# The first loads and the first products of a two-layer encoder kernel: x in 256-column pieces on ScalarE's queue, and another order of the first transposes and products

## The chip, the core and the metric

The kernel runs on one core of a Trainium2 chip. A core has five engines that matter here: TensorE does the matrix products, VectorE and ScalarE work on tiles elementwise, GpSimd does small odd jobs, and SyncE only issues DMAs. ScalarE can issue DMAs too, from a queue of its own; the profile calls a queue's own work ACTq or SPq. The metric is device time in microseconds (us) of one execution, lower is better, and the kernel must compute what the reference computes.

## The reference

An encoder trunk over one sequence: x has 256 tokens and 1024 channels, float32, and there are two layers. Each layer is a token mixer and a gated MLP, both with a root-mean-square norm ahead and a residual add behind:

```python
for layer in range(DEPTH):
    h = h + _token_mixer(_rmsnorm(h, norm1[layer]), w_in[layer], ...)
    h = h + _conv_ffn(_rmsnorm(h, norm2[layer]), w_up[layer], ...)
return _rmsnorm(h, norm_f)
...
u, q, k, v, g_pool, g_attn = jnp.split(xn @ w_in, SPLITS, axis=-1)
```

What matters for this change is the very first thing that the first layer needs: the attention values v, that is, the normed x times the columns of `w_in[0]` that belong to v. They fall in three groups of 512 columns; the first group is computed while the first data is still arriving.

## The kernel before

**Precision.** TensorE is fed in pairs. Every operand is split in a leading part (rounded to the format that TensorE reads at full rate) and a rest (the operand minus its leading part). A product of two operands is then three products: leading times leading, rest times leading, leading times rest. The code calls them `hh`, `lh` (rest of x, leading weights) and `hl` (leading x, rest of the weights).

**Weights.** The class `Weights` streams all weights through three raw buffers with DMAs on SyncE's queue. Each raw piece is split by one ScalarE instruction (leading part) and one VectorE instruction (rest). For the first values the norm's gains have to be multiplied into the weights as well (`open_next`, lines 251 to 264), so each split there is a multiply with a column of `gcol` per 128 channels: L255 on ScalarE or L261 on VectorE makes the leading part, L256 on VectorE the rest.

**The start, in program order.** `begin` (L367) issues the first DMAs. x's tokens are held as two halves t = 0 and 1 of 128 tokens (`h[:, t, :]`). A `part_of_x(t, n)` loads 128 tokens by 512 columns, 256 KB. `next(first)` issues one of four pieces of 256 KB of the first weights, each holding 128 channels by 512 columns. So SyncE's queue holds, in this order: x of t = 0, columns 0 to 511; weight piece 0; x of t = 1, columns 0 to 511; weight pieces 1, 2, 3; x's columns 512 to 1023 for t = 0 and 1; two pieces of 512 KB of the next weights. On ScalarE's queue there is one small DMA, the norm's gains as eight rows of 128 (`grows`, 4 KB, L371).

TensorE meanwhile runs "warm" products of ones (`warm`, L398) whose widths are in `WARM`: six of 128 columns, then the small product that turns `grows` into the column form `gcol` (L392, VectorE copies it at L393), then one of 64 columns. Such a product of ones shows as two instructions in the profile.

Then `begin_values_of_x` (L754) works in an order written out by hand (`manual_schedule`): every engine runs its instructions in the order of the program lines. `turn_x(ts, c0, n)` transposes n blocks of 128 columns of x for the token halves `ts` on TensorE (L774) and returns `keep`, which copies the result out of PSUM as leading part (ScalarE, L780) and rest (VectorE, L781). `split(k)` and `both(k)` split weight piece k. `products((t, k, kinds))` issues products of token half t with weight piece k (L826), 128 by 512 each. The order before:

1. transpose two blocks of t = 0; two more warm products (128 and 64 columns)
2. VectorE: leading part of weight piece 0; copies of the two blocks; product `hh` of t = 0
3. transpose two blocks of t = 1; VectorE: rest of weight piece 0; product `lh` of t = 0; copies of t = 1's blocks
4. transpose the next two blocks of both halves; split weight piece 1
5. `hl` of t = 0, then `hh`, `hl`, `lh` of t = 1, all with piece 0; then the pieces 1, 2, ... for both halves

Behind that come the two other value groups (L919), the rest of the layer and the second layer; none of it is touched.

Of the kernel before, what the change touches and what calls it, by code (L numbers as in the profile page):

```python
# [16 lines left out]
P = 128  # L17
# [16 lines left out]
NT = 5  # L34


WARM = ((P,) * 6, (P // 2,), (P, P // 2))
POOLS = {("q", 1): (2, 2), ("k", 1): (0, 2)}
GROUPS = (("u", 1), ("u", 0), ("q", 0), ("k", 0), ("q", 2), ("k", 2), ("q", 1), ("k", 1))
NQ = NF // 4  # L40
# [12 lines left out]
HALVES = (slice(0, 512), slice(512, D))  # L53
# [227 lines left out]
def encoder(ctx, tc, x, w_in, w_pool, pool_scale, w_a, w_b, w_o, norm1, norm2, w_up, conv_w,  # L281
            conv_b, w_down, rel_bias, norm_f, onehot, edges, out):
    nc = tc.nc
# [70 lines left out]
    h = const.tile([P, 2, D], F32, name="h")  # L354
    xv = x[0].rearrange("(m t) d -> m t d", t=2)
# [11 lines left out]
    def begin():  # L367


        rows8 = sm.tile([KD, P], F32, tag="gain", bufs=1, name="grows")  # L370
        nc.scalar.dma_start(out=rows8, in_=norm1[0].rearrange("(k p) -> k p", p=P))  # L371
        first, second = W.load_by(4), W.load_by(2)

        def part_of_x(t, n):
            nc.sync.dma_start(out=h[:, t, HALVES[n]], in_=xv[:, t, HALVES[n]])

        part_of_x(0, 0)
        next(first)
        part_of_x(1, 0)
        for _ in range(3):  # L380
            next(first)
        part_of_x(0, 1)
        part_of_x(1, 1)
        for _ in range(2):
            next(second)
        W.load(4)
        ones = nc.const_aps.tensor(1.0, (P, P), F32)
        make_identity(nc, ident)
        nc.vector.memset(mhalf, -0.5)
        ps = mmp.tile([P, P], F32, tag="mm", name="gain_ps")  # L390
        warm(ps, ones, WARM[0])
        nc.tensor.transpose(ps[:, 0:KD], rows8, ident[:KD, :KD])  # L392
        nc.vector.tensor_copy(gcol, ps[:, 0:KD])  # L393
        ps = mmp.tile([P, P], F32, tag="mm", name="warm_ps")
        warm(ps, ones, WARM[1])
        return lambda widths: warm(ps, ones, widths)

    def warm(ps, a, widths):  # L398

        for n in widths:  # L400
            nc.tensor.matmul(ps[:, 0:n], a, a[:, 0:n], start=True, stop=True)  # L401
# [281 lines left out]
    def by_tokens(x2, n, at_once=1, then=None, ps=None, begin=0, end=None):  # L683


        if ps is None:
            ps = [mmp.tile([P, 512], F32, tag="mm", name="t_ps") for _ in range(2)]
        for i0 in range(begin, n if end is None else end, at_once):
            held = [W.get() for _ in range(at_once)]
            for t in range(2):  # L690
                for i, piece in enumerate(held, i0):
                    v_sum(ps[t], x2, t, i, piece, n - 1)
            for i, _ in held:
                W.free(i)
            if then:
                then()
        return ps
# [56 lines left out]
    def begin_values_of_x():  # L754


        more = begin()
        W.gains = gcol

# [7 lines left out]
        def turn_x(ts, c0, n):  # L767


            ks = slice(c0, c0 + n)  # L770
            pt = mmp.tile([P, n, len(ts), P], F32, tag="mm", name="xt_ps")
            for j, t in enumerate(ts):
                for k in range(n):
                    nc.tensor.transpose(  # L774
                        pt[:, k, j, :], h[:, t, (c0 + k) * P : (c0 + k + 1) * P], ident
                    )
            tt = slice(ts[0], ts[-1] + 1)

            def keep():
                nc.scalar.copy(out=xuh[:, ks, tt, :], in_=pt)  # L780
                nc.vector.tensor_sub(  # L781
                    out=xul[:, ks, tt, :], in0=pt, in1=xuh[:, ks, tt, :].bitcast(F32)
                )

            return keep
# [29 lines left out]
        def split(k):  # L815
            if k % 2 == 0:
                pieces.append(W.n_split)
                chunks[k], chunks[k + 1] = W.open_next()
            return chunks[k]

        def product(t, k, kind):
            wh, wl = W.split[pieces[k // 2]]
            a, w = {"hh": (xuh, wh), "lh": (xul, wh), "hl": (xuh, wl)}[kind]
            first = k == 0 and kind == "hh"
            last = k == KD - 1 and kind == ("lh" if t else "hl")
            return nc.tensor.matmul(ps[t], a[:, k, t, :], w[:, k % 2, :], start=first, stop=last)  # L826

        def both(k):

            hi, lo, _ = split(k)  # L830
            hi()
            return lo()

        def products(*steps):
            for t, k, kinds in steps:
                for kind in kinds:
                    last = product(t, k, kind)
            return last

        every = ("hh", "lh", "hl")  # L840
        keep = turn_x((0,), 0, 2)
        more(WARM[2])
        _, lo, hi = split(0)
        hi()
        keep()
        products((0, 0, ("hh",)))
        keep = turn_x((1,), 0, 2)
        lo()
        products((0, 0, ("lh",)))
        keep()  # L850
        keep = turn_x((0, 1), 2, 2)
        both(1)
        products((0, 0, ("hl",)), (1, 0, ("hh", "hl", "lh")))
        keep()
        both(2)
        products((0, 1, ("hh", "lh")), (1, 1, ("hh", "lh")), (0, 1, ("hl",)), (1, 1, ("hl",)))
        both(3)
# [5 lines left out]
        keep = turn_x((0,), 4, 4)  # L863
# [3 lines left out]
        keep = turn_x((1,), 4, 4)  # L867
# [59 lines left out]
    for l in range(DEPTH):  # L927
# [21 lines left out]
        if l == 0:  # L949
            with tc.manual_schedule():  # L950
                begun = begin_values_of_x()
            x2 = first_values(*begun, keep_values)
        else:
            for g in range(NG):
                held = begun[0] if g == 0 else [W.get() for _ in range(4)]
                for t in range(2):
                    if g + t == 0:
                        ps = begun[1]
                    else:
                        ps = v_tile()  # L960
                        for n in range(4):
                            v_sum(ps, x2, t, n, held[n])
                    keep_values(t, g, ps)
                for i, _ in held:
                    W.free(i)
# [81 lines left out]
        def pool_out():  # L1047
            for j in (1, 0):
                if j:
                    po2 = got["po2"] = two_parts("m2", "po2")  # L1050
                i, (wh, wl) = W.get()
                for gg in range(2):
                    ps = [mmp.tile([P, 2, S], F32, tag="mm", name="pool_ps") for _ in range(2)]
                    for oc in range(2):
                        cc = slice(oc * P, (oc + 1) * P)
                        two_sums(
                            pooled[2 * j + gg], 2,
                            (ps[oc], lambda k: wh[:, 2 * gg + k, cc], lambda k: wl[:, 2 * gg + k, cc]),
                        )
                    if gg:  # L1060
                        W.free(i)
                    po = [sm.tile([P, 2, P], F32, tag="u", name="po") for _ in range(2)]
                    first = 4 * j + 2 * gg
                    for oc in range(2):
                        sc = hps[:, l, first + oc : first + oc + 1]
                        nc.scalar.mul(out=po[oc], in_=halves(ps[oc][:, 1]), mul=sc)
                    for oc in range(2):
                        sc = hps[:, l, first + oc : first + oc + 1]
                        nc.vector.scalar_tensor_tensor(
                            out=po[oc], in0=halves(ps[oc][:, 0]), scalar=sc, in1=po[oc],  # L1070
                            op0=ALU.mult, op1=ALU.add,
                        )
                    yield
                    for oc in range(2):
                        nc.scalar.copy(out=po2[:, first + oc, 0], in_=po[oc])
                    for oc in range(2):
                        c = first + oc
                        nc.vector.tensor_sub(out=po2[:, c, 1], in0=po[oc], in1=po2[:, c, 0].bitcast(F32))
                    yield
# [21 lines left out]
        products = pool_out()  # L1101
# [136 lines left out]
        with tc.manual_schedule():  # L1238
# [27 lines left out]
            first = None  # L1266
            for n, cc in enumerate(HALVES):
# [13 lines left out]
                first = []  # L1281
                for t in range(2):
                    nc.vector.scalar_tensor_tensor(
                        out=th[:, t], in0=th[:, t], scalar=1.0, in1=ps[t], op0=ALU.add, op1=ALU.mult
# [196 lines left out]
```

## Time and profile before

| | |
|---|---|
| median of three runs | 856.17 us (854.75, 856.17, 856.28) |
| the profiled execution, its own time | 855.71 us |
| its span, from the first to the last instruction | 853.9 us |
| TensorE busy | 99% of the span, 3927 products |
| VectorE, ScalarE, GpSimd busy | 73%, 57%, 4% |
| DMA | 214.03 MB moved, 251 GB/s in the mean |

The 1.8 us between the profiled execution's time and its span lie ahead of the first and behind the last instruction. "PE" is TensorE's products and "PEld" its weight loads, DVE is VectorE, ACT ScalarE, POOL GpSimd. In a row of the timeline the first number is the start in us from the span's start, the second the time during which the row's instructions ran; "x4" is their count, and what stands in brackets is the engine's idle time ahead of the row and what ended it. Products are pipelined, so that the duration of one (0.39 us for 512 columns) is longer than the distance between the starts of two. A row of the chain of waits is a stretch of the path that ended last: start, length, and on what it was spent.

### The profile page before, as it was taken

What the parts mean: (1) busy time and instruction counts of PE and PEld (TensorE: products, weight loads), DVE (VectorE), ACT (ScalarE), POOL (GpSimd) and SP (SyncE); (2) the same over time, 40 slices, a digit from 0 to 9 for tenths busy, and PEclk for the clock granted to TensorE, in tenths of its full rate; (3) what the DMA queues carried; (4) which work ended last, traced back from release to release, by engine and by line L of the source; (5) the groups of instructions that cost most, each with busy time, mean ns of one, the idle gap of its engine ahead of it and who ended that gap; (6) DMA issues with size and microseconds to landing.
All of it is one profiled execution on the core that took longest, in us unless ns stands there. A gap on an engine that the chain in (4) does not pass through costs nothing.

```text
span 853.9 us, 11004 instructions
## 1 busy us (share of the span) xinstructions
PE 846.6 (99%) x3927; PEld 707.7 (83%) x3927; DVE 620.5 (73%) x883; ACT 488.5 (57%) x720; POOL 33.1 (4%) x98
## 2 busy tenths in 40 slices
PE   9999999999999999999999999999999999999997
PEld 7888888888888888888888888888888888888885
DVE  6958777757766877878655687868577767777774
ACT  6645556654544765657545454577454556556662
POOL 1800000000010000000000000000000100000001
PEclk9999999999999999999999999999999999999999
DMA  8599987785657979997726899869777489699941
GB/s 320 197 313 278 303 282 249 252 280 212 223 216 263 308 233 302 290 286 240 243 102 209 262 280 326 252 220 264 243 265 266 141 301 305 230 288 288 301 141 50
DMA packets 147406, 214.03 MB, mean 251 GB/s; under 512 B 7752, under 2 KB 68240, under 8 KB 147352
## 3 DMA queue, kind: packets, MB, share of 16 engines
q1 hardware_dynamic: 147192, 213.13, 76.5%
q8 instruction: 31, 0.51, 0.2%
q14 instruction: 23, 0.19, 0.1%
q10 hardware_dynamic: 160, 0.20, 0.1%
HBM read 186.02 MB, written 27.28 MB: 250 GB/s over the span
## 4 chain that ended last, share of the span: by engine, by line
PE 99%; DMA 0%; POOLq 0%; ACT 0%; issue 0%; DVE 0%; DVEq 0%; POOL 0%; ACTq 0%
PE t_ps L678 64%; PE v_ps L678 6%; PE res_ps L597 6%; PE res_ps L595 6%; PE res_ps L596 6%; PE v_ps L919 3%; PE v_ps L826 1%; PE pool_ps L582 1%; PE o_ps L1189 1%; PE s_ps L1141 1%; PE s_ps L1136 1%; PE o_ps L1185 1%; PE xt_ps L520 1%; DMA h<-in_x_dram 0%; PE xt_ps L774 0%; PE warm_ps L401 0%
## 5 line engine op out<-in xcount | busy, mean ns | idle before, releaser
L245 DVE TENSOR_TENSOR wl<-raw,wh 128x1024 fp32r<-128x1024 f32 x274 | 332.0, 1221 | 160.4 <-ACT wh L243 159.6
L678 PE MATMUL t_ps<-wh,x 128*128 128x512 f32 x1408 | 439.0, 390 | 0.0
L243 ACT CAST wh<-raw 128x1024 fp32r<-128x1024 f32 x274 | 286.4, 1052 | 216.7 <-PE t_ps L678 149.3
L678 PEld LDWEIGHTS t_ps<-wh,x 128*128 128x128 f32 x1408 | 264.3, 188 | 54.8
L678 PE MATMUL t_ps<-wl,x 128*128 128x512 f32 x704 | 273.9, 389 | 0.0
L678 PEld LDWEIGHTS t_ps<-wl,x 128*128 128x128 f32 x704 | 132.2, 188 | 27.3
L597 PE MATMUL res_ps<-wh,actk 128*128 128x512 f32 (+1 forms) x184 | 70.0, 380 | 0.0
L595 PE MATMUL res_ps<-wh,actq 128*128 128x512 f32 (+1 forms) x184 | 69.9, 380 | 0.0
L596 PE MATMUL res_ps<-wl,actq 128*128 128x512 f32 (+1 forms) x184 | 69.9, 380 | 0.0
L678 PE MATMUL t_ps<-wh,po 128*128 128x512 f32 x128 | 41.4, 395 | 0.0
L596 PEld LDWEIGHTS res_ps<-wl,actq 128*128 128x128 f32 x184 | 34.6, 188 | 6.6
L597 PEld LDWEIGHTS res_ps<-wh,actk 128*128 128x128 f32 x184 | 34.6, 188 | 6.6
L595 PEld LDWEIGHTS res_ps<-wh,actq 128*128 128x128 f32 x184 | 34.6, 188 | 6.5
L485 POOL TENSOR_SCALAR ss<-ss 128x1 f32<-128x1 f32 x8 | 2.2, 280 | 774.4 <-ACT junk L478 774.4
L678 PEld LDWEIGHTS t_ps<-wh,po 128*128 128x128 f32 x128 | 24.1, 188 | 4.9
L1362 ACT ACTIVATE y<-a,prm 128x256 f32<-128x256 f32 x44 | 26.5, 602 | 1.5
L595 PE MATMUL res_ps<-wh,m 128*128 128x512 f32 (+1 forms) x72 | 26.5, 367 | 0.0
L596 PE MATMUL res_ps<-wl,m 128*128 128x512 f32 (+1 forms) x72 | 26.3, 365 | 0.0
L728 DVE STREAM_TRANSPOSE crossing<-t_ps 128x512 f32<-128x512 f32 x40 | 26.1, 691 | 0.0
L597 PE MATMUL res_ps<-wh,m 128*128 128x512 f32 (+1 forms) x72 | 26.0, 366 | 0.0
L678 PE MATMUL v_ps<-wh,x 128*128 128x512 f32 x80 | 25.7, 392 | 0.0
L678 PE MATMUL t_ps<-wl,po 128*128 128x512 f32 x64 | 24.9, 390 | 0.0
(189 smaller groups left out, 932.1 us busy)
## 6 DMA issues: line engine op xcount, KB each, us to landing
raw<-in_w_in_dram SPq DMA_DIRECT2D x58, 1024.0 KB, 6.4
raw<-in_w_up_dram SPq DMA_DIRECT2D x40, 1024.0 KB, 8.7
raw<-in_w_down_dram SPq DMA_DIRECT2D x22, 1024.0 KB, 5.6
crossing<-crossing SPq DMA_DIRECT2D x22, 512.0 KB, 6.0
crossing<-way SPq DMA_DIRECT2D x16, 512.0 KB, 4.9
raw<-in_w_a_dram SPq DMA_DIRECT2D x8, 1024.0 KB, 6.3
raw<-in_w_o_dram SPq DMA_DIRECT2D x8, 1024.0 KB, 7.1
zga<-crossing SPq DMA_DIRECT2D x40, 128.0 KB, 4.0
```

The costliest lines, as they stand in the source:

```text
L243: inst = nc.scalar.copy(out=h, in_=src)
L245: inst = self.rests[i] = nc.vector.tensor_sub(out=l, in0=src, in1=h.bitcast(F32))
L520: nc.tensor.transpose(pt[:, k, :], xn[:, c0 : c0 + P], ident)
L582: nc.tensor.matmul(out, w(k), x, start=(steps is first and k == 0), stop=(steps is last and k == nk - 1), skip_group_check=turns["rest"],)
L595: nc.tensor.matmul(ps, ah, wh, start=first, stop=False, skip_group_check=on)
L596: nc.tensor.matmul(ps, ah, wl, start=False, stop=False, skip_group_check=on)
L597: nc.tensor.matmul(ps, al, wh, start=False, stop=last, skip_group_check=on)
L678: nc.tensor.matmul(ps, x2[:, 2 * n + j, part, t, :], w[:, j, :], start=(n + m == 0), stop=(n == last and m == 5),)
L728: nc.vector.transpose(out=y[:, t].rearrange("p q c j -> p c q j"), in_=rows[t])
L826: return nc.tensor.matmul(ps[t], a[:, k, t, :], w[:, k % 2, :], start=first, stop=last)
L919: nc.tensor.matmul(ps[t], a[:, k, t, :], w[:, j, :], start=(k + m == 0), stop=(k == KD - 1 and m == 2),)
L1362: nc.scalar.activation(y, a, AF.Identity, bias=b, scale=w1)
```

## The change

x's first 256 columns are loaded for both token halves as two DMAs of 128 KB on ScalarE's queue; SyncE's queue begins with weight piece 0. The gains (`grows`) move from ScalarE's queue to SyncE's, behind weight piece 0. Columns 256 to 511 of both halves follow as one DMA of 256 KB behind weight piece 1. Then come the weight pieces 2 and 3 and the two DMAs of columns 512 to 1023, as before. The warm products behind the gains' product become three of 64 columns. Both halves' first two blocks are transposed ahead of the two further warm products; the products are `hh` and `lh` of both halves, then the transposes of the next two blocks, then `hl` of both. In the instructions of each engine this moves VectorE's copy of t = 0's rest ahead of the leading part of weight piece 0, and its copy of t = 1's rest ahead of the rest of piece 0. A long way behind, one 1 MB load on SyncE's queue (L165) comes after two small parameter loads (L413, L414) and not before them. Everything else keeps its order.

```diff
-WARM = ((P,) * 6, (P // 2,), (P, P // 2))
+WARM = ((P,) * 6, (P // 2,) * 3, (P, P // 2))
...
         rows8 = sm.tile([KD, P], F32, tag="gain", bufs=1, name="grows")
-        nc.scalar.dma_start(out=rows8, in_=norm1[0].rearrange("(k p) -> k p", p=P))
         first, second = W.load_by(4), W.load_by(2)
 
-        def part_of_x(t, n):
-            nc.sync.dma_start(out=h[:, t, HALVES[n]], in_=xv[:, t, HALVES[n]])
-
-        part_of_x(0, 0)
+        def part_of_x(queue, t, cc):
+            queue.dma_start(out=h[:, t, cc], in_=xv[:, t, cc])
+
+        for t in range(2):
+            part_of_x(nc.scalar, t, slice(0, 256))
         next(first)
-        part_of_x(1, 0)
-        for _ in range(3):
+        nc.sync.dma_start(out=rows8, in_=norm1[0].rearrange("(k p) -> k p", p=P))
+        next(first)
+        part_of_x(nc.sync, slice(0, 2), slice(256, 512))
+        for _ in range(2):
             next(first)
-        part_of_x(0, 1)
-        part_of_x(1, 1)
+        for t in range(2):
+            part_of_x(nc.sync, t, HALVES[1])
...
         keep = turn_x((0,), 0, 2)
+        keep()
+        keep = turn_x((1,), 0, 2)
         more(WARM[2])
         _, lo, hi = split(0)
         hi()
         keep()
-        products((0, 0, ("hh",)))
-        keep = turn_x((1,), 0, 2)
         lo()
-        products((0, 0, ("lh",)))
-        keep()
+        products((0, 0, ("hh", "lh")), (1, 0, ("hh", "lh")))
         keep = turn_x((0, 1), 2, 2)
         both(1)
-        products((0, 0, ("hl",)), (1, 0, ("hh", "hl", "lh")))
         keep()
+        products((0, 0, ("hl",)), (1, 0, ("hl",)))
         both(2)
```

## The prediction

> **What bounds the kernel now.** The page comes first, then the mean over the stages behind the start, then the chain of waits for the first 9 us.
>
> ```profile
> span 853.9 us, 11004 instructions
> ...
> PE 846.6 (99%) x3927; PEld 707.7 (83%) x3927; DVE 620.5 (73%) x883; ACT 488.5 (57%) x720; POOL 33.1 (4%) x98
> ...
> PE 99%; DMA 0%; POOLq 0%; ACT 0%; issue 0%; DVE 0%; DVEq 0%; POOL 0%; ACTq 0%
> ```
>
> ```profile
> 10.00:15.00 5.00, 5.00 (x28) 4.08 (x26) 4.37 (x9) 3.98 (x10) 2.23 (x6) 1.00 1.06 410
> 15.00:20.00 5.00, 5.00 (x23) 3.98 (x22) 5.00 (x8) 5.00 (x9) 0.00 (x0) 1.00 1.07 395
> ```
>
> ```profile
> 0.72 3.87 DMA h<-in_x_dram
> 4.59 0.04 issue
> 4.63 0.69 PE xt_ps L774 x2
> 5.32 0.75 PE warm_ps L401 x4
> 6.07 0.12 issue
> 6.19 0.77 PE v_ps L826
> 6.96 0.43 PE xt_ps L774 x2
> 7.38 0.43 PE v_ps L826
> 7.81 0.64 PE xt_ps L774 x4
> 8.45 0.70 PE v_ps L826 x3
> ```
>
> TensorE's products are 99% of the chain that ends last. In the stages from 10 to 20 us PE (the first number behind the stretch's length) is busy for 5.00 of 5.00 us. From the first saturated product on nothing else ends a wait, so a shift of that point passes to the end one for one. Only the first 8 us have room: the chain starts with x's DMA for 3.87 us (issued at 0.72, landed at 4.59), and until 8.45 us TensorE waits or runs short work: 4.63 transposes, 5.32 warm products, 6.19 the first real product.
>
> How fast TensorE runs there decides what a shift is worth:
>
> ```profile
> 0.76 2.90 PE L401 MATMUL gain_ps<-const-float32-1.0 128*128 128x128 f32 x12 [0.76 <-PEq L1463]
> ...
> 3.59 0.27 PE L392 MATMUL gain_ps<-ident,grows 8*128 8x8 f32 x1
> ...
> 7.04 0.78 PE L826 MATMUL v_ps<-m,xul 128*128 128x512 f32 x1
> ...
> 7.61 0.84 PE L774 MATMUL xt_ps<-ident,h 128*128 128x128 f32 x4
> ...
> 8.21 0.95 PE L826 MATMUL v_ps<-m,xuh 128*128 128x512 f32 x3
> ...
> 8.99 0.40 PE L826 MATMUL v_ps<-m,xul 128*128 128x512 f32 x1
> ...
> 9.22 0.39 PE L826 MATMUL v_ps<-m,xuh 128*128 128x512 f32 x1
> ...
> 11.52 0.60 PE L774 MATMUL xt_ps<-ident,h 128*128 128x128 f32 x4
> ```
>
> A product of 512 columns lasts 0.78 us at 7.04 and 0.40 us at 8.99; four transposes last 0.84 us at 7.61 and 0.60 us at 11.52. The starts at 8.99 and 9.22 are 0.23 us apart, the fast rate; I take twice that, 0.47 us, for the slow one. So up to about 8.1 us TensorE runs at half its rate, and from there at the full one (the column of the granted clock, behind the busy times in the stages' rows, reads 1.00 in the slow stretch too; the durations decide). By 9.22 the kernel before has done six products (the ones at 6.19 and 7.04, three from 8.21, one at 8.99) and the first eight transposes. That is the mark against which I measure.
>
> **The change part by part.** The sum is made against the profiled execution's own 855.71 us (span 853.9); the median of the runs is 856.17, 0.46 above it.
>
> *What a microsecond at the start is worth.* Let S be the start of the first real product. In the changed order all behind it is ready early (below), so six products and four transposes follow without a pause: at the slow rate 6 x 0.47 + 4 x 0.19 = 3.58 us, at the full one 6 x 0.23 + 4 x 0.11 = 1.82 us (0.19 from the 0.84 us row, 0.11 from the 0.60 us row, each less a last product of 0.27, as at 3.59, and over three steps). With the rate doubling at 8.1 us, they end at 8.1 + (1 - (8.1 - S)/3.58) x 1.82. That equals 9.22 for S = 6.72. So the difference is 0.5 x (S - 6.72), since what is done early is done at half rate. Before, S was 6.19, but with waits in what followed.
>
> *The gains' DMA on the other queue.* This is the costliest edit.
>
> ```profile
> L392 PEldq EVENT_SEMAPHORE  x1: 51/51/51, 2.3 to 2.3; - x1
> ```
>
> ```profile
> 0.72 0.58 ACTq L371 DMA_DIRECT2D grows<-in_norm_dram  x1
> ...
> 0.72 0.38 SPq L375 DMA_DIRECT2D h<-in_x_dram  x1
> ...
> 1.16 0.42 SPq L184 DMA_DIRECT2D raw<-in_w_in_dram  x1
> 1.34 1.28 ACT L780 ACT_TABLE_LOAD   x1 [1.34 <-PEq L1463]
> 1.63 0.42 SPq L375 DMA_DIRECT2D h<-in_x_dram  x1
> ...
> 3.79 0.69 PE L401 MATMUL warm_ps<-const-float32-1.0 128*128 128x64 f32 x2
> ...
> 5.56 0.48 DVE L261 TENSOR_SCALAR m<-raw,gcol 128x512 fp32r<-128x512 f32 x1 [1.50 <-DMA raw<-in_w_in_dram]
> ```
>
> Before, the gains were alone on ScalarE's queue: issued at 0.72, and the wait for them in TensorE's queue (the row at 2.3) was over by 2.4 us, long before L392 ran at 3.59. Now they are issued on SyncE's queue behind weight piece 0, from 1.16 on, and their rows stand behind that piece's. TensorE stops at L392 until they land, at a time G. Bounds: 2.8 us if they pass as freely as before (2.4 plus the 0.44 us that the issue is later), and 5.5 us, where before the first two 256 KB pieces of SyncE's queue had landed (the wait that ended at 5.56). The nearest row is x's own piece, first on that queue, landed at 4.59. The gains are only eight rows, so they need not wait for the slowest part; I take 4.3.
>
> *The warm products.* The three of 64 columns stand behind L392 and ahead of the transposes, so they run after G. From L392 to the next product pass 0.2 us (3.59 to 3.79). The wider ones run at 2.90/12 = 0.24 us an instruction, so six narrow ones take between half of that and all of it, 0.7 to 1.4 us (the pair at 3.79 lasted 0.69 with its drain); I take 1.1, and so the transposes start at T = G + 1.3 = 5.6 us, if x is there. With G at 2.8 they would hide behind x's DMA and cost nothing.
>
> *x on ScalarE's queue.* Two DMAs of half the size start beside weight piece 0. Their landing isn't in this trace; bounds are 2.4 us (the gains on that queue) and 5.5 us (512 KB through both queues, the same bytes as before the 5.56 of weight piece 0). I take 4.4 for t = 0, nearest to the 4.59 of x's piece, and 5.2 for t = 1; before, t = 1 came much later:
>
> ```profile
> h<-in_x_dram SPq DMA_DIRECT2D x1, 256.0 KB, 4.9
> ```
>
> 1.63 + 4.9 = 6.5 us, which is the wait ahead of the transposes at 6.76 (the chain's 6.96 row). This wait goes; what is late next is G. ScalarE's second issue (0.58 us, as L371's) pushes its table load from 1.34 to about 2 us; that costs nothing, as the engine sits idle until 5.36.
>
> ```profile
> 1.50:2.50 1.00, 1.00 (x7) 1.00 (x6) 0.00 (x0) 1.00 (x1) 0.00 (x0) 1.00 0.36 111
> ...
> 4.50:5.50 1.00, 0.87 (x4) 0.87 (x5) 0.00 (x0) 0.14 (x1) 0.00 (x0) 1.00 0.94 291
> ```
>
> The second last column is the DMA engines' busy share, the last GB/s. From 4.5 us on they are 94% busy whichever queue feeds them; only in the first microsecond (0.36) is there room. [...]
>
> *From the transposes to the first product.*
>
> ```profile
> 5.36 0.37 ACT L780 CAST xuh<-xt_ps 128x256 fp32r<-128x256 f32 x1 [2.74 <-PE xt_ps L774]
> ...
> 5.96 0.42 DVE L781 TENSOR_TENSOR xul<-xt_ps,xuh 128x256 fp32r<-128x256 f32 x1
> ...
> 6.30 0.74 DVE L256 SCALAR_TENSOR_TENSOR m<-raw,gcol,m 128x512 fp32r<-128x512 f32 x1
> ...
> 7.69 0.73 ACT L255 ACTIVATE m<-raw,gcol 128x512 fp32r<-128x512 f32 x1
> ```
>
> ScalarE's copy started 0.73 us behind the first transpose (4.63 to 5.36) and took 0.37; VectorE's leading part of piece 0 (0.48) ran at 5.56 beside it (row above), and its copy of the rest (0.42) behind, at 5.96. The product started 0.15 behind L261's end (6.04 to 6.19). Now L781's copy is ahead of L261: 0.73 + 0.37 + 0.03 + 0.42 + 0.48 + 0.15 = 2.2 us from T to S, where it was 1.56. So S = 5.6 + 2.2 = 7.8 us. What follows is covered: t = 1's copies end at about S, piece 0's rest (0.74 at L256) 0.8 us later and is needed four products later (1.9 us slow, 0.9 fast); piece 1's leading part (0.73) started at 7.69 before and now has no need before S + 2. Without that cover, each product waits for VectorE, some 0.4 us once.
>
> *Sum.* 0.5 x (7.8 - 6.72) = +0.54 us. On top, the doubling itself: it came 3.5 us behind the start of the near-gapless work at 4.63 (8.1 - 4.63). TensorE now rests from 3.5 to G and begins later, so I let the doubling be 0.4 us later on average: +0.2. Total +0.74: 855.71 + 0.74 = 856.45, rounded **856.5 us**.
>
> *The queue behind.*
>
> ```profile
> 12.86 0.31 SPq L413 DMA_DIRECT2D prow<-in_conv_b_dram  x1
> ...
> 13.21 0.36 SPq L414 DMA_DIRECT2D prow<-in_pool_scale_dram  x1
> ```
>
> SyncE still issues eight DMAs ahead of the 512 KB pieces. The swap of one 1 MB load with two small ones costs at most 0.31 + 0.36 us of issue, and nothing as long as TensorE is gapless behind (stages above).
>
> **The rivals.**
>
> *The data comes early.* G at 3.3 or less and x's first piece at 4.2 to 4.6: T = 4.2 to 4.6, S = 6.4 to 6.8, -0.2 to 0.0 us, so 855.5 to 855.7. For it: the early room in the DMA engines, and t = 1's wait gone. Against: x's piece alone took until 4.59, and now it shares the engines with weight piece 0.
>
> *Slower: the doubling comes much later.* TensorE's pause for G interrupts the warm products, and the run-up begins anew. Before, 7.3 us passed from the first warm product (0.76) to 8.1; counted again from G = 4.3 that is 11.6, 3.5 us later, and costs 0.5 x 3.5 = 1.75 on top of 0.54: 858.0 us. With G = 5.5 (S = 9.0, doubling 1.2 us later) it is 1.1 + 0.6 = +1.7, 857.4. It decides from the point where the pause ahead of L392 is over a microsecond (G above 4.5). [...]
>
> *Faster: the doubling comes earlier.* [...] With x at 4.2, S is about 6.0, the ten steps end at 7.82, -1.4 us: 854.3. Against: in the trace the six warm products from 0.76 to 3.66 did not suffice.
>
> [...]
>
> **How the numbers follow.** Forecast (T between 5.0 and 6.2, whether by G or by the shared DMA engines) 0.50, at +0.3 to +1.2, 856.0 to 856.9; early data 0.25; doubling much later 0.20; doubling earlier 0.05. With the runs' own spread added, the range is 855.0 to 858.0; it leaves out the last case and what is slower still. 0.2%, about what a measurement of this kernel can tell from no change, is 1.7 us: no case but the last gains nearly that from 855.71 (854.3 lies below 856.17 by more), and of the slow one, 857.4 to 858.0, I count all. Faster 0.05, same 0.75, slower 0.20.
>
> **What would show it.** Right: the L392 row starts well behind 3.59 us, with TensorE idle ahead of it; the transposes at 5.6; the first product at 7 to 8 us, and from there no wait; the mark of 9.22 reached at about 9.8. Wrong: L392 still at 3.6 (then the gains are not what counts); x's two pieces both landed before 4 us; or the 0.4 us products beginning far from 8.1 us, in either direction, since the moment of the doubling moves the time by half of its own shift.

## The result, and the profile after

The changed kernel takes 857.87 us (median of 16 runs, 857.22 to 858.55); the kernel before, on the same chip, 855.79 (16 runs, 854.58 to 856.65). The ratio is 1.0025, with a 95% interval of 1.0018 to 1.0033: slower by a quarter of a per cent. The forecast was 856.5 with a range of 855.0 to 858.0. The time lies inside the range, at its upper edge (7 of the 16 runs lie above 858.0), but the case that came is not the likeliest one: it is the rival in which the doubling of TensorE's rate comes much later, priced at 858.0. The profiled execution took 858.05 us, 2.34 more than the one of before (855.71).

The page of the changed kernel, its busy times and the shares of its chain, and the means of its stages behind the start:

```profile
span 856.2 us, 11014 instructions
...
PE 848.2 (99%) x3931; PEld 709.2 (83%) x3931; DVE 620.6 (72%) x883; ACT 488.8 (57%) x720; POOL 32.8 (4%) x98
...
PE 99%; DMA 0%; issue 0%; DVE 0%; ACT 0%; POOLq 0%; SPq 0%; DVEq 0%; POOL 0%; ACTq 0%
```

```profile
10.00:15.00 5.00, 5.00 (x24) 4.24 (x23) 3.26 (x7) 3.52 (x8) 0.94 (x4) 1.00 1.05 403
15.00:20.00 5.00, 5.00 (x25) 3.91 (x24) 4.63 (x7) 4.61 (x9) 1.27 (x3) 1.00 1.01 383
```

As before, TensorE's products are 99% of the chain, and from 10 us on PE is busy for 5.00 of 5.00 us. Nothing is lost or won behind the start, so the 2.34 us must lie in the first 12 us. The chain of waits of the changed kernel there:

```profile
1.17 3.20 DMA grows<-in_norm_dram
4.37 0.14 issue
4.50 0.24 PE gain_ps L394
4.74 1.47 PE warm_ps L403 x6
6.21 0.44 PE xt_ps L776 x2
...
6.68 0.38 ACT xuh L782
...
7.42 0.49 DVE m L261
7.91 0.14 issue
8.05 2.04 PE v_ps L828 x4
10.09 0.85 PE xt_ps L776 x4
```

It no longer begins with x: behind the issue of weight piece 0 (0.72 to 1.11) come the gains, issued at 1.17, landed 3.20 us later, at 4.37. Then come the small product L394, the three narrow products of ones (two instructions each, "x6") for 1.47 us, the transposes, ScalarE's copy, VectorE's leading part of weight piece 0 and, at 8.05, the first real product. From there on no wait follows. The products one by one, from the timeline:

```profile
4.50 0.24 PE L394 MATMUL gain_ps<-ident,grows 8*128 8x8 f32 x1 [0.84 <-DMA grows<-in_norm_dram]
4.67 1.54 PE L403 MATMUL warm_ps<-const-float32-1.0 128*128 128x64 f32 x6
6.01 1.06 PE L776 MATMUL xt_ps<-ident,h 128*128 128x128 f32 x4
...
8.05 0.77 PE L828 MATMUL v_ps<-m,xuh 128*128 128x512 f32 x1 [0.23 <-DVE m L261]
...
9.47 0.63 PE L828 MATMUL v_ps<-m,xul 128*128 128x512 f32 x1
...
10.60 1.37 PE L828 MATMUL v_ps<-m,xuh 128*128 128x512 f32 x3
11.81 0.39 PE L828 MATMUL v_ps<-m,xul 128*128 128x512 f32 x1
```

The bracket in the first row is the pause: TensorE stood 0.84 us for the gains. The last rows are the larger matter. A product of 512 columns still lasts 0.63 us at 9.47; at 11.81 one lasts 0.39. So the rate doubled at about 11.5 us, where it had done so at about 8.1 before. The mark of the prediction, six products and eight transposes done, is the start of the seventh product; it was 9.22 and is now 11.58, where the third of the three products at 10.60 starts (0.23 ahead of the one at 11.81). That is 2.36 us later, and the profiled times differ by 2.34: the whole slowdown is behind TensorE by 11.6 us.

The stages around the pause and around the first product:

```profile
3.50:4.50 1.00, 0.16 (x1) 0.03 (x1) 0.00 (x0) 0.00 (x0) 0.00 (x0) 1.00 1.07 392
...
7.50:8.50 1.00, 0.77 (x3) 0.61 (x3) 1.00 (x4) 0.60 (x1) 0.00 (x0) 1.00 0.92 234
```

TensorE (first number behind the length) was busy for 0.16 us of the stage from 3.5 us and for 0.77 us of the one from 7.5 us.

### The profile page after: what moved, and what is told of

It is laid out like the page before. It is cut to its first block, busy times and chain, and to the rows that moved or that the text cites. A ratio compares the mean times of both kernels' runs of the same rounds, so it can differ in the third digit from the quotient of the medians.

```text
span 856.2 us, 11014 instructions
## 1 busy us (share of the span) xinstructions
PE 848.2 (99%) x3931; PEld 709.2 (83%) x3931; DVE 620.6 (72%) x883; ACT 488.8 (57%) x720; POOL 32.8 (4%) x98
## 4 chain that ended last, share of the span: by engine, by line
PE 99%; DMA 0%; issue 0%; DVE 0%; ACT 0%; POOLq 0%; SPq 0%; DVEq 0%; POOL 0%; ACTq 0%
PE t_ps L680 64%; PE v_ps L680 6%; PE res_ps L599 6%; PE res_ps L598 6%; PE res_ps L597 6%; PE v_ps L920 3%; PE v_ps L828 1%; PE pool_ps L584 1%; PE o_ps L1190 1%; PE s_ps L1142 1%; PE s_ps L1137 1%; PE o_ps L1186 1%; PE xt_ps L522 1%; DMA grows<-in_norm_dram 0%; PE xt_ps L776 0%; PE warm_ps L403 0%
```

## The experiments

The theory after this reading, my estimate from the two traces: the price is the moment of the doubling (11.5 us for 8.1; half of that shift is 1.7 of the 2.1 us), and the pause for the gains with the thin work around it puts it off. The rivals: the idle stretch of the pause does so alone (the pause theory); the later first product itself is the price (the late-start theory: order and waits, whatever the rate does); or the loads behind it are, since x's pieces and the weights now share the first microseconds. The expectations below describe the kernels and give times of the rivals. Kernels 1 to 4, 5 to 8 and 9 to 12 ran together, beside 30, 30 and 33 runs of the kernel before (medians 855.96, 856.09 and 855.90). Where only widths or counts of the products of ones differ, nothing of the output changes.

In the tables, S is the start of the first real product, C the moment of the doubling (the time stamp of the trace's first record of the granted clock; the durations of the products change there) and M the mark.

### 1. The gains back on ScalarE's queue

```diff
+        nc.scalar.dma_start(out=rows8, in_=norm1[0].rearrange("(k p) -> k p", p=P))
...
-        nc.sync.dma_start(out=rows8, in_=norm1[0].rearrange("(k p) -> k p", p=P))
```

> [...] Late-start theory (the doubling is luck; what counts is the first product's start, 8.05 against 6.19, and each microsecond of it costs a whole one): first product 0.6 us later than before, 856.4. Third theory (the new order of products and the pieces of x cost something of their own): 857 or more.

Measured: 858.44 us (857.59 to 859.70), ratio 1.0031 (1.0020 to 1.0041). By its time that is the third theory's case (857 or more), but the profile shows another reason. The timeline of this kernel:

```profile
3.59 0.27 PE L394 MATMUL gain_ps<-ident,grows 8*128 8x8 f32 x1
...
6.19 0.69 PE L776 MATMUL xt_ps<-ident,h 128*128 128x128 f32 x2 [0.85 <-DMA h<-in_x_dram]
7.37 0.69 PE L776 MATMUL xt_ps<-ident,h 128*128 128x128 f32 x2 [0.49 <-DMA h<-in_x_dram]
```

The pause is gone: L394 ran at 3.59 as before. But x's first piece, now behind the gains on ScalarE's queue (issued at 1.34, where it had been 0.72), landed at 6.14 and its second at 7.32 (4.36 and 4.71 in the changed kernel), so the transposes waited at 6.19 and 7.37, S came at 8.56 and the doubling at 11.9. Of the first piece's 16 parts 15 had landed by 5.09, and one took until 6.14; weight piece 1 beside it had 15 parts by 4.41 and the last at 5.94. Why, no run settles. The kernel says nothing on the gains' place by itself; number 7 does.

### 2. The pause filled

```diff
-WARM = ((P,) * 6, (P // 2,) * 3, (P, P // 2))
+WARM = ((P,) * 8, (P // 2,) * 3, (P, P // 2))
```

> The changed kernel with eight warm products of 128 columns in place of six, so that the pause ahead of the gains' product shrinks from 1.05 us to about 0.2 and nothing else moves. [...] Late-start theory: the first product is where it was, so nothing changes: 857.9 (+2.1).

Measured: 857.43 us, ratio 1.0011 (1.0002 to 1.0021). The median hides two groups: five runs at 855.35 to 856.05, six at 857.43 to 858.68, nothing between; the 856.2 that a doubling back at 8.1 us would give (857.87 less 1.7) is in neither. The profiled run is one of the second group:

```profile
4.94 0.24 PE L394 MATMUL gain_ps<-ident,grows 8*128 8x8 f32 x1 [0.42 <-DMA grows<-in_norm_dram]
...
11.04 1.59 PE L828 MATMUL v_ps<-m,xuh 128*128 128x512 f32 x3
12.46 0.40 PE L828 MATMUL v_ps<-m,xul 128*128 128x512 f32 x1
```

The pause is halved (0.42 us for 0.84 by the profile's idle time; the 1.05 us of the expectation counts from the last column streamed), and still the rate doubled only at 12.5 us in this run. The gains landed at 4.80 here, 0.43 later than in the changed kernel, so S moved as well, to 8.48. So the pause alone doesn't decide; with it halved, about half of the runs double early, to judge by their times (only one was profiled), where none of the 16 runs of the changed kernel did.

### 3. The kernel before with fewer products of ones

```diff
-WARM = ((P,) * 6, (P // 2,), (P, P // 2))
+WARM = ((P,) * 3, (P // 2,), (P, P // 2))
```

> The kernel before with three warm products in place of six ahead of the gains' product: a pause of TensorE of some 1.5 us between about 3.0 and 4.6, with every DMA, the transposes at 4.63 and the first product at 6.19 where they were. [...] Late-start theory: no difference, 855.8.

Measured: 856.18 us (855.49 to 857.73), ratio 1.0007 (0.9998 to 1.0016), which is no difference that can be told. C came at 8.8 (8.1 before). The median shows no late doubling, though three of the 11 runs reach 856.96 to 857.73. What is gone is a group of runs: of the 93 runs of the kernel before beside the experiments, 21 lie at 854.58 to 855.00 and none between there and 855.59; none of these 11 lies in the lower group. So the kernel before seems to owe that group to its six products of ones, though in its profiled run the rate did not double behind them. Eleven runs would miss a group of that size by luck about once in seventeen times.

### 4. The order alone

The kernel before with nothing but the changed order of `begin_values_of_x` (its loads and products of ones as before).

> The kernel before with the changed kernel's order of transposes and products alone; DMAs and warm products as before. The second half's transposes wait for x until 6.5 us, the first product comes at about 7.8. [...] Late-start theory: +1.6 for the first product's shift, 857.4, with the doubling where it was.

Measured: 857.53 us (855.33 to 858.04), ratio 1.0015 (1.0006 to 1.0023). In the timeline the second pair of transposes waits for x's second piece, as the loads are the old ones:

```profile
6.46 0.69 PE L774 MATMUL xt_ps<-ident,h 128*128 128x128 f32 x2 [1.23 <-DMA h<-in_x_dram]
```

S is 7.66 (6.19 before), C 9.6, M 10.48 (+1.26). On the old loads the order costs mostly by that wait: 1.23 us in which TensorE streams nothing, and a first product and a doubling that are each 1.5 us later. The late-start theory's 857.4 fits the median, but it had left the doubling where it was.

### 5 and 6. Products of ones as wide as they go

```diff
-WARM = ((P,) * 6, (P // 2,) * 3, (P, P // 2))
+WARM = ((512,) * 4, (512,), (512,))
```

That is number 5, on the changed kernel; number 6 is the kernel before with

```diff
-WARM = ((P,) * 6, (P // 2,), (P, P // 2))
+WARM = ((512,) * 3, (512,), (512,))
```

> The changed kernel with its narrow warm products replaced by wide ones of 512 columns (four ahead of the gains' product, one behind it, one behind the transposes); DMAs and order as changed. [...] Late-start theory: first product where it was, 857.9.

> The kernel before with wide warm products of 512 columns (three, one, one) in the places of the narrow ones; nothing else. [...] Pause theory and late-start theory: TensorE is no busier than it was by the clock on the wall and the first product stays at 6.19: 855.8, no difference.

Measured: 5 857.84 us (857.20 to 858.71), ratio 1.0026 (1.0016 to 1.0036); 6 856.23 (855.89 to 857.25), 1.0006 (0.9997 to 1.0015). The 857.9 of the late-start theory fits number 5, and number 6 is no difference that can be told, as both rivals had it (855.8), but not for their reason: in neither did the first product stay where it was. The timeline of 5:

```profile
0.76 6.08 PE L403 MATMUL gain_ps<-const-float32-1.0 128*128 128x512 f32 x8 [0.76 <-PEq L1464]
...
9.67 0.47 PE L828 MATMUL v_ps<-m,xuh 128*128 128x512 f32 x1 [0.32 <-ACT m L255]
```

The rate doubled at 5.6 us (6.7 in 6), six microseconds earlier than in the changed kernel. But eight instructions of 512 columns last 6.08 us, far past the gains' landing, and the real work waits behind them: S is 9.67 (8.31 in 6). What the doubling brought, the late S took back. So the doubling can be had early in both kernels, and is worth nothing if it is bought with products that overrun.

### 7 and 8. The gains first on SyncE's queue

```diff
+        nc.sync.dma_start(out=rows8, in_=norm1[0].rearrange("(k p) -> k p", p=P))
         first, second = W.load_by(4), W.load_by(2)
...
         next(first)
-        nc.sync.dma_start(out=rows8, in_=norm1[0].rearrange("(k p) -> k p", p=P))
```

The gains stand ahead of weight piece 0, not behind it. 8 has `WARM = ((512,) * 3, (512,), (512,))` as well.

> The changed kernel with the gains' DMA ahead of weight piece 0 on SyncE's queue, and nothing else: gains land at about 2.5, x's pieces at 4.4 to 4.8, transposes at 4.8, first product at 6.9. Pause and late-start theories: the loss is gone but for 0.1 to 0.4 us: 855.8 to 856.3. [...]

> Both: the gains first on SyncE's queue and wide warm products (three, one, one) in the changed kernel. [...]

Measured: 7 856.55 us (854.68 to 856.95), ratio 1.0005 (0.9997 to 1.0014), above the 855.8 to 856.3 of the pause and the late-start theory; 8 856.91 (856.38 to 857.62), 1.0014 (1.0005 to 1.0023). In 7 too there are two groups: three runs at 854.68 to 855.05, eight at 856.13 to 856.95, with the profiled run among the eight. Its timeline:

```profile
3.59 0.27 PE L394 MATMUL gain_ps<-ident,grows 8*128 8x8 f32 x1
3.79 1.54 PE L403 MATMUL warm_ps<-const-float32-1.0 128*128 128x64 f32 x6
5.12 1.06 PE L776 MATMUL xt_ps<-ident,h 128*128 128x128 f32 x4
...
7.16 0.77 PE L828 MATMUL v_ps<-m,xuh 128*128 128x512 f32 x1 [0.23 <-DVE m L261]
```

The gains land at 2.29, the pause is gone, and of the changed kernel's 2.08 us over the kernel before 0.46 are left, by moving one 4 KB load by one place. The rate still doubles only at 9.5 us; the three narrow products and the gap ahead of the first product are still there. In 8 it doubles at 5.0, and again the wide products push S to 8.54.

### 9. The kernel before with a dense start

```diff
-WARM = ((P,) * 6, (P // 2,), (P, P // 2))
+WARM = ((P,) * 6, (224,), (320,))
```

The widths are chosen to fill TensorE's time up to x's landing and between the transposes and the first product, and no further.

> The kernel before with its two gaps filled: one warm product of 224 columns (3.79 to 4.54) in place of 64, and one of 320 (5.06 to 6.1) in place of 128 and 64; DMAs, order, transposes at 4.6 and first product at 6.1 to 6.2 stay. [...] If density doesn't matter: 855.8 to 856.1 with the spread of before.

Measured: 854.80 us (854.58 to 854.94), ratio 0.9989 (0.9980 to 0.9998). The spread of the 11 runs is 0.36 us, against 2.05 of the kernel before beside it (854.64 to 856.69).

```profile
3.79 0.80 PE L401 MATMUL warm_ps<-const-float32-1.0 128*128 128x224 f32 x2
4.46 0.44 PE L774 MATMUL xt_ps<-ident,h 128*128 128x128 f32 x2
4.73 0.71 PE L401 MATMUL warm_ps<-const-float32-1.0 128*128 128x320 f32 x2
6.30 0.47 PE L826 MATMUL v_ps<-m,xuh 128*128 128x512 f32 x1 [0.86 <-DVE m L261]
```

At 6.30, where the first product starts (6.19 before), the rate is already doubled: that product lasts 0.47 us, where it took 0.77 before. C is 4.1, M 8.47 (0.75 earlier; the profiled time is 0.80 less). All 11 runs lie where the lower group of the kernel before lies (854.58 to 855.00, see number 3).

### 10. The changed kernel with a dense start

```diff
-WARM = ((P,) * 6, (P // 2,) * 3, (P, P // 2))
+WARM = ((P,) * 8, (384,), (P, P))
```

Loads and order are those of the changed kernel.

> The changed kernel with its gaps filled and nothing put off: eight warm products ahead of the gains' product, one of 384 columns (same 1.28 us as the three of 64, but dense) behind it, two of 128 behind the transposes; DMAs and order as changed, the transposes still held by the gains. [...] If the late first product is what costs: 857.0 or more.

Measured: 856.35 us (855.69 to 857.56), ratio 1.0006 (0.9998 to 1.0015). C is 4.1, S 7.59, M 9.50 (+0.28). The median lies below the 857.0 that the late first product would have cost. Products of ones, which compute nothing, bring the changed kernel from 2.08 us over the kernel before to 0.45, though the gains land even later in the profiled run (4.79 for 4.37). That run took 857.0, 1.29 more than the one of before, of which the mark explains 0.28. Its chain of waits shows the rest:

```profile
5.79 8.08 DMA raw<-in_w_in_dram
...
13.90 0.73 ACT ybig L255
...
14.66 0.76 DVE ybig L256
...
15.46 1.56 PE v_ps L828 x5
```

A piece of the next weights landed only at 13.87; its split held up the products at 14.68, 15.02 and 15.46. In number 9 the same split began at 11.87, with no wait behind it. So beyond the mark the weights' arrival is the next limit; why it was late in this run is open.

### 11. The loads alone

The kernel before with the changed kernel's loads; its order and `WARM` as before.

> The changed kernel's DMAs alone (x in pieces on ScalarE's queue, gains behind weight piece 0), with the order and the warm products of before. The gains land at 4.4, the transposes start at about 5.2, the first product at 6.7, and the wait for the second half of x is gone. [...] If the loads are harmless: 855.8.

Measured: 856.50 us (855.08 to 857.37), ratio 1.0008 (1.0000 to 1.0017). The gains landed at 4.71; the pause, from the timeline:

```profile
4.84 0.24 PE L394 MATMUL gain_ps<-ident,grows 8*128 8x8 f32 x1 [1.18 <-DMA grows<-in_norm_dram]
```

S is 6.63, only 0.44 later than before, but C is 9.9, 1.8 later, and M 10.29 (+1.07): the loads cost mostly by the doubling. Loads and order alone move the profiled time by 1.03 and 1.26 us, together 2.29; the changed kernel's is 2.34. In the medians it is 0.60 and 1.57, together 2.17, for 2.08. The change's third part, the three narrow products, was not run by itself.

### 12. The gains first, x at once, no narrow products

```diff
-WARM = ((P,) * 6, (P // 2,) * 3, (P, P // 2))
+WARM = ((P,) * 6, (), (192,))
+        nc.sync.dma_start(out=rows8, in_=norm1[0].rearrange("(k p) -> k p", p=P))
         first, second = W.load_by(4), W.load_by(2)
...
         next(first)
-        nc.sync.dma_start(out=rows8, in_=norm1[0].rearrange("(k p) -> k p", p=P))
...
         keep = turn_x((0,), 0, 2)
-        keep()
-        keep = turn_x((1,), 0, 2)
         more(WARM[2])
+        keep1 = turn_x((1,), 0, 2)
         _, lo, hi = split(0)
         hi()
         keep()
+        keep1()
         lo()
```

> A version made from what the runs showed: gains first on SyncE's queue, x's pieces on ScalarE's (landed at 3.3 to 3.6 and 4.8 in e7 and e8), the first half's transposes at once behind the gains' product at 3.8, one dense warm product of 192 columns until the second half is there, VectorE's leading part of weight piece 0 ahead of x's rests, products as in the changed kernel. First product at 5.3 to 5.5, TensorE dense from 0.76. [...] If the weights' splits and the later pieces of x then hold it up: 855.0 to 855.5.

Measured: 854.63 us (854.22 to 855.88), ratio 0.9988 (0.9979 to 0.9997). It is faster than both kernels (number 9 can't be told from it), and the change's own idea, x beside the first weights and both halves' transposes ahead, is in it.

```profile
3.79 0.69 PE L776 MATMUL xt_ps<-ident,h 128*128 128x128 f32 x2
4.27 0.85 PE L403 MATMUL warm_ps<-const-float32-1.0 128*128 128x192 f32 x2
4.91 0.63 PE L776 MATMUL xt_ps<-ident,h 128*128 128x128 f32 x2
5.30 0.77 PE L828 MATMUL v_ps<-m,xuh 128*128 128x512 f32 x1
...
6.72 0.40 PE L828 MATMUL v_ps<-m,xul 128*128 128x512 f32 x1
```

The transposes stand right behind the gains' product, at 3.79, as x's first piece landed at 3.4; the first product starts at 5.30, 2.75 us ahead of the changed kernel's, and the rate doubles at 6.7. M is 7.86 (1.36 earlier; the profiled time is 1.37 less). So x beside the first weights and the early transposes need be no loss. Number 12 differs from the changed kernel in three things, though: the gains' place, the products of ones, and an order in which VectorE's leading part of weight piece 0 stands ahead of x's rests again. How much each of them brings, it doesn't tell.

### What they say together

The prediction's rule for the stretch was: from S on, six products and four transposes, 3.58 us at the slow rate or 1.82 at the full one. With the measured S and C it gives the mark of every kernel in the changed order:

| kernel | S | C | mark by the rule | M measured | M less 9.22 | profiled time less 855.71 |
|---|---|---|---|---|---|---|
| changed kernel | 8.05 | 11.5 | 11.6 | 11.58 | +2.36 | +2.34 |
| 1 gains back | 8.56 | 11.9 | 12.0 | 12.01 | +2.79 | +2.80 |
| 2 pause filled | 8.48 | 12.5 | 12.1 | 12.04 | +2.82 | +2.97 |
| 4 order alone | 7.66 | 9.6 | 10.4 | 10.48 | +1.26 | +1.26 |
| 5 wide | 9.67 | 5.6 | 11.5 | 11.58 | +2.36 | +2.31 |
| 7 gains first | 7.16 | 9.5 | 10.2 | 10.17 | +0.95 | +0.84 |
| 8 gains first, wide | 8.54 | 5.0 | 10.4 | 10.44 | +1.22 | +1.18 |
| 10 dense | 7.59 | 4.1 | 9.4 | 9.50 | +0.28 | +1.29 |
| 12 early start | 5.30 | 6.7 | 7.8 | 7.86 | -1.36 | -1.37 |

Two numbers, S and C, fix the mark within 0.1 us, and the mark fixes the time within 0.15 us but for number 10, whose rest was found above. In the kernels of the old order there are waits behind S, so the rule doesn't give their mark, but the mark gives their time as well: +0.28 and +0.24 in number 3, +1.39 and +1.54 in 6, -0.75 and -0.80 in 9, +1.07 and +1.03 in 11. The rival that the loads behind the start are the price falls with this table. The rival that S alone is the price falls too: kernels 2 and 8 have the same S within 0.1 us and differ by 1.6 us in the mark, and by 1.79 in profiled time.

What sets C was not shown. The traces show this much: in the eight kernels whose products of ones have at most 128 columns C is 8.1 to 12.5; in the six that have wider ones (192 to 512 columns, numbers 5, 6, 8, 9, 10 and 12) it is 4.1 to 6.7. But the work ahead of it doesn't fix it: numbers 2 and 10 run the same sixteen instructions of 128 columns from 0.76 us on, and in 10 the rate doubled at 4.1 us, before they were through (4.39) and ahead of any wider product, in 2 at 12.5. Nor does the pause: number 7 has none and doubles at 9.5. So the moment moves from run to run, and one profiled execution of each kernel doesn't tell how often it comes early.

The runs' times tell a little more. In the early group lie 21 of the 93 runs of the kernel before, 5 of 11 in number 2, 3 of 11 in number 7, one of 11 in number 4, none of the 16 of the changed kernel, none of 11 in number 3, and all 11 in number 9. (The runs of 1 and 11 form no clear groups.) That the early doubling comes the more often, the more of the first microseconds TensorE streams columns, is my estimate from these counts: number 3, with half the products of ones, has no early run, number 2, with a third more of them, has 5, and number 9, with the gaps filled, has nothing else. No run shows how it comes about.

Each part of the changed kernel leaves TensorE less to stream there. The gains' pause takes 0.84 us out. The six instructions of the narrow products last 1.54 us with a drain of about 0.27, as the row at 4.67 shows: 0.21 us each, while the twelve of twice the columns took 2.90, 0.22 each. The first narrow instruction behind wider ones took 0.11 us (7.29 to 7.40), so I estimate that about half of the others' time is empty. The row of their weight loads points to why:

```profile
4.67 1.35 PEld L403 LDWEIGHTS warm_ps<-const-float32-1.0 128*128 128x128 f32 x6
```

Each loads 128 by 128 weights for its 64 columns, six in 1.35 us, 0.23 us each; ahead of the 128 columns twelve such loads take 2.64 us, 0.22 each. Then TensorE rests 0.23 us ahead of the first product, where VectorE now has one copy more to do.

## Why the prediction was right or wrong

- **What bounds it, and what a shift is worth: right.** Behind the start nothing moved, and with S = 8.05 and the doubling left at 8.1 the prediction's 0.5 x (S - 6.72) is +0.67. It had +0.54.
- **The gains' DMA: right.** Forecast G = 4.3, measured 4.37. Numbers 7 and 12 show that it need not be: first on the queue they land at 2.2 to 2.3.
- **The narrow products: 0.2 us short.** Forecast 1.1 us, measured 1.34 (4.67 to 6.01), so they take nearly the full time of the wider ones (0.22 us an instruction), the upper bound that I had written beside it. T is 6.01 for 5.6.
- **x on ScalarE's queue: right for the first piece, cautious for the second.** 4.36 and 4.71, forecast 4.4 and 5.2; weight piece 0 landed at 4.52 (5.45 in the kernel before). Neither decided: T waited for the narrow products. That the shared DMA engines deliver x's two pieces and weight piece 0 together, near 5.5, and so set T, which the forecast's 0.50 allowed beside G, no run shows: in the changed kernel the last of them landed at 4.71, though it was issued no earlier (1.14) than the second 256 KB of the kernel before (1.16, landed at 5.45). In the other profiled executions with these loads it was 4.83 to 5.14 (numbers 2, 5, 10 and 11), against 5.22 to 5.70 with the old ones (3, 4, 6 and 9). Number 1, with the same spread over two queues, had x at 6.14 and 7.32, so how far the spreading did it stays open.
- **From the transposes to the first product: right.** 2.04 us, forecast 2.2; S = 8.05, forecast 7.8. No wait behind it, as forecast.
- **The doubling: wrong, and the whole miss.** The step was "so I let the doubling be 0.4 us later on average: +0.2". It came 3.4 us later, 11.5 for 8.1, which by the same rule is worth 11.58 - 9.22 - 0.67 = 1.7 us. The sum +0.74 should have been +2.36.
- **The rival that came, and its condition.** "The doubling comes much later", with 11.6 us and 858.0, is what happened, to 0.1 us. That the 11.6 fits so closely is luck: it came from counting 7.3 us anew from the gains' landing, and no such count holds elsewhere (number 3 pauses 1.29 us ahead of 4.49 and doubles at 8.8; number 7 doesn't pause and doubles at 9.5; number 9 doesn't pause there either and doubles at 4.1). Its chance was 0.20, and its condition was misread: it was to decide only with G above 4.5 and a pause over a microsecond, a point that was my estimate and that no run shows. G was 4.37 and the pause 0.84, and number 2 halves the pause and keeps the late doubling in half of the runs. The time lies inside the range only because the range counted this rival in. Number 7, without the pause, still doubles at 9.5. That all the time counts in which TensorE streams nothing, the narrow products' idle halves and the gap ahead of the first product included, is the estimate above; the prediction counted these instructions as busy.
- **A run's luck: not in this kernel.** The prediction added the runs' own spread to its range, with three runs from 854.75 to 856.28. For the kernel before that holds, with 16 runs from 854.58 to 856.65. All 16 runs of the changed kernel lie at 857.22 to 858.55: by their times, the rate doubles early in none.
- **The early doubling (0.05): dismissed for a wrong reason.** That "in the trace the six warm products from 0.76 to 3.66 did not suffice" holds for that one execution; in a fifth of the runs, by their times, they did. With two wider ones behind them (number 9) all 11 runs lie at the early time, and the profiled one has C at 4.1.

## What to carry to other kernels

TensorE's first microseconds are worth what they do to the moment at which its rate doubles: half of the shift, here 1.7 us, twice the 0.84 us of the pause itself. So fill them with wide products that end when the data comes, as number 9 does (not narrow ones, which took 0.21 us an instruction for 64 columns where 128 took 0.22; not ones that overrun, as in numbers 5, 6 and 8), and put no load that TensorE's first in-order work needs behind a larger one (the gains landed at 4.37 behind weight piece 0, at 2.29 ahead of it). Before a start is reordered, add up for how long TensorE streams columns in it, before and after.

## What was not expected of the hardware

- The doubling came anywhere from 4.1 to 12.5 us in 14 profiled executions, on nearly the same work. The granted clock of the stages reads 1.00 ahead of it as behind; only the durations (0.63 and 0.39 us for 512 columns) show it.
- In a row of them, a product of ones with 64 columns costs about as much as one with 128, 0.21 and 0.22 us an instruction at the slow rate. The first narrow instruction behind wider ones took 0.11 us (7.29 to 7.40 in the changed kernel).
- Where x's first piece stands beside the gains moves its landing, though the gains are only 4 KB: 3.61 us with the gains first on SyncE's queue (number 7), 4.36 with them behind weight piece 0, 6.14 with them ahead of x on ScalarE's own queue (number 1). Number 1 has one straggling part of 16 at that; the cause is open.
